# A hybrid convolution and S5 layer on one core: gelu in halves behind the sigmoids, one more buffer for each part of the gate, layer norms three to four steps earlier

## Chip, core and metric

The kernel runs on one core of a Trainium2 chip. The metric is the device time of one execution in microseconds (us). The kernel before has a median of 1850.74 us over three runs (1848.5 to 1852.46). TensorE (PE) does the matmuls, VectorE (DVE), ScalarE (ACT) and GpSimd (POOL) the elementwise work; SyncE (SP) issues every transfer (DMA) named here, one after the other. Each engine takes its instructions strictly in the order in which the program has them.

## What is computed

2048 positions of width 1024. The reference, cut to what matters here (the projections in front and the S5 scan itself are left out):

```python
p = split(h @ w_in)                       # val, glu gate, silu gate, u, silu gate: 5 x 1024 columns
# convolution branch
v = p0 * sigmoid(p1)
v = dwconv_latent(v, w, bias)             # 31 taps on a grid
v = silu(layernorm(v, ln_g, ln_b))
conv_out = v * silu(p2)
# S5 branch
y = gelu(y_f + y_b + d * u)               # y_f, y_b: the two scans, forwards and backwards
y = y * sigmoid(y @ glu_w + glu_b)
ssm_out = y * silu(p4)
mix = concat(conv_out, ssm_out) @ w_out
x = x + gate * mix
return rmsnorm(x, final_g)
```

## The kernel before

Activations lie with channels on the 128 partitions: 1024 channels are 8 channel tiles (`ct` or `k`, 0 to 7), and the positions are 4 blocks of 512 (`nb`). Each fp32 product is made of three passes: both operands are split in a high and a low part, and `mm3` (L133, L138, L139) adds high by high, high by low and low by high. A **product** below is 8 such triples, 24 matmuls of 512 columns, into one PSUM bank. All matmuls stand in one hand-made chain, each product's first one tied behind the last of the product before (`last`, `chain`), so that PE's order is the order of the code.

The stages follow each other: input projection with the convolution beside it (0 to about 700 us), S5 scan (to about 1243 us) with the last silu gates' columns projected between its parts, Glu stage (to 1436.6 us) and output stage (to the end).

- **End of the S5 stage.** For each group of channels ACT copies the transposed input operand `E` out of PSUM (L859), PE multiplies `S` from it (L892), DVE makes the state `H` (L904 to L927), PE reads it out as `Y` (L934, L943), and `ys` is written to DRAM as `y_d` (L947, L951). `activated(nb, ks)` loads channel tiles `ks` of `y_d` for one block (L1014), two to a buffer, applies gelu (L1021), rounds the high part `yh` (L1022) on ACT and makes the low part `yl` (L1023) on DVE. For block 0 that load has one buffer, for the others two. The silu gates leave PSUM as `gs` (L445).
- **Glu stage.** `project` makes one product `yh, yl` by `gwh, gwl` into `ps`, `gated(ct, nb, ps)` finishes it: loads the silu gate `gg` (L1112), adds `yf` = `yh` + `yl` (L1115), multiplies by `gg` (L1116), takes the sigmoid of `ps` into `gsg` on ACT (L1118), multiplies (L1119) and stores to `mix_d` (L1120). `ps` has few PSUM banks, so a product waits until an earlier `gsg` has read its bank. In block 0 the first five tiles (`EARLY`) project all but the last `k`, then the last one. The eight gelus of block 1 stand ahead of ct 5 of block 0, those of blocks 2 and 3 behind ct 1 of the block before.
- **Layer norms.** `layer_norm(nb)` is a generator of four steps: load `lx` and sum it on POOL (L1031 to L1036, `lsum`); the mean `mu` by a matmul (L1039), subtraction (L1042), squares (L1044, L1047) that POOL adds up (L1048, `lsq`); the variance `va` (L1052) and its inverse root `dg` on DVE; the root spread over the partitions `rb` (L1063), normalisation (L1068), silu (L1070), times the gate `lg` loaded pair by pair into one buffer (L1076, L1077), store to `mix_d` (L1078). The steps of block 0 run in the Glu stage behind the steps 8 * nb + ct named in `LN_STEPS`; those of blocks 1 to 3 in the output stage, four position tiles `t_` each, behind the half tiles of `LN_HALF`.
- **Output stage.** `w_out(i)` loads a row tile `wor` (L1000), rounds `woh` on ACT (L1001), and makes `wol` on POOL or DVE (L1002). Each position tile `t_` (16 of them) has four products `pso`: its S5 half (k8 = 1) times two column halves, then its convolution half. `mix_in` loads `mr` (L1097), `split_mix` makes `mh` on ACT (L1103) and `ml` on DVE (L1104). `evacuate` multiplies by the gate `gbc` and adds the input (L1177, L1178), `finish` applies the final norm with `fg` (L1189) and stores.

Order: the code runs under `tile.TileContext(schedule_with_timeline_sim=True)`, so a scheduler decides how ACT, DVE, POOL and SP interleave, within data dependencies and the hand-made ties.

Of the kernel before, what the change touches and what calls it, by code (L numbers as in the profile page):

```python
# [7 lines left out]
F32 = mybir.dt.float32  # L8
F32R = mybir.dt.float32r
I32 = mybir.dt.int32  # L10
AF = mybir.ActivationFunctionType
ALU = mybir.AluOpType
MUL, ADD, SUB = ALU.mult, ALU.add, ALU.subtract

P = 128
# [7 lines left out]
KT = D // P  # L23
NB = SEQ // 512
# [5 lines left out]
ROWS = SEQ // GRIDW  # L30
EPS = 1e-6

LN_STEPS = (6, 12, 16, 19)

LN_HALF = (0, 2, 4, 5)

H_LAST = (0, 2, 1, 3)

EARLY = 5
# [14 lines left out]
S_C, S_NG, S_BA, S_DW, S_DB, S_LG, S_LB, S_GB, S_D = 0, 16, 24, 48, 296, 304, 312, 320, 328  # L54
# [25 lines left out]
def build(ctx: ExitStack, tc: tile.TileContext, ins: dict, out: bass.AP):  # L80
# [705 lines left out]
    with tc.tile_pool(name="ss", bufs=2, reuse_waits="tile") as s2p, tc.tile_pool(name="ss1", bufs=1, reuse_waits="tile") as s1p, \  # L786
# [35 lines left out]
        def inputs(b):  # L822

            g0 = G * b
            gs_ = slice(g0, g0 + G)
            h2 = slice((b % 2) * G, (b % 2) * G + G)
            if b % 2 == 0:
                B_ = KBs[b // 2]
                KB = KBs[b // 2] = [s2p.tile([P, 4, GH], F32, tag=f"KB{i}", name=f"KB{i}") for i in range(2)]
                kt = s1p.tile([P, 4, GH], F32, tag="kt", name="kt")  # L830
                a = kbr[:, g0:g0 + 4].unsqueeze(2).to_broadcast([P, 4, GH])
                c = kbi[:, g0:g0 + 4].unsqueeze(2).to_broadcast([P, 4, GH])
                pt(KB[0], B_[0], a, op=MUL)
                pt(kt, B_[1], c, op=MUL)
                pt(KB[0], KB[0], kt, op=SUB)
                pt(KB[1], B_[0], c, op=MUL)
                pt(kt, B_[1], a, op=MUL)
                pt(KB[1], KB[1], kt, op=ADD)
            KB = KBs[b // 2]
            l = [t_[:, gs_].unsqueeze(3).to_broadcast(shp) for t_ in (lre, lim)]  # L840
            a = [t_[:, h2].unsqueeze(2).to_broadcast(shp) for t_ in KB]
            X = [s1p.tile(shp, F32, tag=f"X{i}", name=f"X{i}") for i in range(2)]
            xp = s1p.tile(shp, F32, tag="xp", name="xp")
            pt(X[0], a[0], l[0], op=MUL)
            pt(xp, a[1], l[1], op=MUL)
            pt(X[0], X[0], xp, op=SUB)
            pt(X[1], a[0], l[1], op=MUL)
            pt(xp, a[1], l[0], op=MUL)
            pt(X[1], X[1], xp, op=ADD)
            et = mm.tile([P, G, 2, P], F32, tag="mm", name="et")  # L850
            for g in range(G):
                for i in range(2):
                    m = nc.tensor.transpose(et[:, g, i], X[i][:, g].rearrange("p j h -> p (j h)"), ident)
                    if g == 0 and i == 0:
                        chain(m)
            last[0] = m
            k = blk[b]
            k.E = s1p.tile([P, G, 2, P], F32, tag="E", name="E")
            act(k.E, et, AF.Copy)  # L859

        def frame(b):

# [141 lines left out]
    def activated(nb, ks=range(KT)):  # L1004

        for k in ks:
# [11 lines left out]
                y_, (hi, lo) = y2[:, k % 2], yy[k, nb]  # L1018
            else:
                continue  # L1020
            act(y_, y_, AF.Gelu_apprx_tanh)  # L1021
            act(hi, y_, AF.Copy)  # L1022
            vt(lo, y_, hi.bitcast(F32), op=SUB)  # L1023

# [83 lines left out]

    def gated(ct, nb, ps):

        gt = gp.tile([P, 512], F32, tag="gg", name="gg")
        nc.sync.dma_start(gt, sg_d[ct][:, nb * 512:(nb + 1) * 512])  # L1112
        yf = gp.tile([P, 512], F32, tag="yf", name="yf")
        hi, lo = yy[ct, nb]
        vt(yf, hi.bitcast(F32), lo.bitcast(F32), op=ADD)  # L1115
        vt(yf, yf, gt, op=MUL)  # L1116
        sg = gp.tile([P, 512], F32, tag="gsg", bufs=1, name="gsg")
        act(sg, ps, AF.Sigmoid, bias=sml[:, S_GB + ct:S_GB + ct + 1])  # L1118
        vt(yf, yf, sg, op=MUL)  # L1119
        nc.sync.dma_start(mixed(nb, KT + ct), yf.rearrange("p (t q) -> p t q", q=P))  # L1120
        if 8 * nb + ct in LN_STEPS:
            next(lns[0])
# [12 lines left out]
    activated(0, [KT - 1])  # L1135
    for ct in range(EARLY):
        gated(ct, 0, project(gw[ct], yy, 0, [KT - 1], pss[ct]))
    activated(1)
    for ct in range(EARLY, KT):
        gated(ct, 0, project(gw[ct], yy, 0))  # L1140
    for nb in range(1, NB):
        for ct in range(KT):
            gated(ct, nb, project(gw[ct], yy, nb))
            if ct == 1 and nb + 1 < NB:
                activated(nb + 1)
            if nb == 2 and ct == 0:
                gbc = lp.tile([P, 1024], F32, name="gbc")
                fg = lp.tile([P, 1024], F32, name="fg")
                nc.sync.dma_start(gbc, gate_d[0:1].broadcast_to([P, 1024]))
                for row in (gate_d[1:2], ins["b_gate"]):  # L1150
                    nc.sync.dma_start(fg, row.broadcast_to([P, 1024]))
                    vt(gbc, gbc, fg, op=ADD)
                nc.sync.dma_start(fg, ins["final_g"].broadcast_to([P, 1024]))
            if nb == NB - 1:
                if ct == 0:
                    first = {hf: split_mix(mix_in(0, hf), hf) for hf in (1, 0)}
# [9 lines left out]
    with tc.tile_pool(name="op", bufs=2, reuse_waits="tile") as op:  # L1166
# [14 lines left out]
        def finish(t_, cols, xt, sq):  # L1181
# [6 lines left out]
            for cs_ in [slice(0, 1024)] if t_ < 15 else [slice(0, 512), slice(512, 1024)]:  # L1188
                st(xt[:, cs_], xt[:, cs_], rs, fg[:, cs_], op0=MUL, op1=MUL)  # L1189
                nc.sync.dma_start(ov[row(t_)[0], row(t_)[1], cs_], xt[:, cs_])  # L1190

        mrs = [None, None]
        for t_ in range(16):
            pool = mm if t_ % 2 == 0 else ops
# [15 lines left out]
            for k8 in (1, 0):  # L1210
# [6 lines left out]
                if t_ < 15:  # L1217
                    for i in range(2):
                        product(k8, i)
                        if k8 == 0:  # L1220
                            evacuate(i, cols[i], pss[i], xt, sq)
                if t_ < 12 and 2 * (t_ % 4) + 1 - k8 in LN_HALF:
                    next(lns[t_ // 4 + 1])
            if t_ == 15:
                for i in range(3):
                    product(1, i)
# [78 lines left out]
```

## Time and profile before

| | |
|---|---|
| median of three runs (lowest, highest) | 1850.74 us (1848.5, 1852.46) |
| the profiled execution | 1840.61 us, span 1838.8 us |
| PE busy | 1729.1 us, 94% of the span |
| DVE, ACT, POOL busy | 1422.2, 588.9, 602.9 us |
| granted TensorE clock, mean | 0.973 |
| Glu stage in the span | 1243 to 1436.6 us |
| output stage in the span | 1436.6 to 1838.8 us |

The span runs from the first to the last instruction; the execution's own time has about 2 us more. PE is close to always busy, so the first thing to look at is what stands between its matmuls: the waits listed for PE, each with the instruction that released it, and the stretches in which the clock column (PEclk, share of full speed) is below 1.00, because a matmul takes longer there.

### The profile page before, as it was taken

Reading aid. Unit: us, or ns where it says so; the run is one execution under the profiler, and the core shown is the slowest. Engines: PE = TensorE matmul, PEld = TensorE weight load, DVE = VectorE, ACT = ScalarE, POOL = GpSimd, SP = SyncE. Lnnn points to the kernel's source line nnn. Section 1 sums busy time; section 2 is a strip of 40 time slices with the busy share of each in tenths; the row PEclk is TensorE's granted clock in tenths of the full one; section 3 lists DMA queues with packets and bytes.
Section 4 is the critical chain, followed back from the end, with each engine's and each line's share of the span. In section 5 each row is a group of like instructions: output and inputs, shape, how many; then the busy total and the mean of one; then the engine's idle time right before and its main releaser. Section 6 shows DMA issues by size and latency. Waiting matters only on the chain.

```text
span 1838.8 us, 23677 instructions
## 1 busy us (share of the span) xinstructions
PE 1729.1 (94%) x8712; PEld 1363.7 (74%) x8712; DVE 1422.2 (77%) x2055; ACT 588.9 (32%) x905; POOL 602.9 (33%) x565
## 2 busy tenths in 40 slices
PE   7799799999999998999999999988999898989998
PEld 2675577787778886777777777777877686877877
DVE  6772799999998897999999999976575565555633
ACT  4442221221122123333443443454444322222211
POOL 1642244343342116556456464302022332213000
PEclk9899899999999998999999999999999999999999
DMA  9604121222222113333333333367549627363431
GB/s 351 211 18 125 33 104 53 94 78 80 69 99 86 57 63 108 116 109 104 111 108 118 114 95 117 101 214 222 148 122 284 225 92 215 106 177 120 130 123 46
DMA packets 175724, 227.45 MB, mean 124 GB/s; under 512 B 38516, under 2 KB 117492, under 8 KB 174584
## 3 DMA queue, kind: packets, MB, share of 16 engines
q1 hardware_dynamic: 175608, 225.94, 38.4%
q8 instruction: 69, 1.13, 0.3%
q14 instruction: 47, 0.39, 0.1%
HBM read 147.36 MB, written 78.52 MB: 123 GB/s over the span
## 4 chain that ended last, share of the span: by engine, by line
PE 53%; DVE 27%; DMA 10%; issue 4%; ACT 3%; SPq 2%; POOL 1%; DVEq 0%; ACTq 0%; POOLq 0%
PE ps L133 9%; PE ps L138 9%; PE ps L139 9%; DVE fQ L336 5%; PE pso L139 4%; PE pso L133 4%; PE pso L138 4%; DVE fR L336 4%; DVE fP L336 4%; PE S L892 3%; DMA mix_d<-yf 3%; DMA lg<-cg_d 3%; PE Y L943 3%; DMA y<-y_d 2%; PE Y L934 1%
## 5 line engine op out<-in xcount | busy, mean ns | idle before, releaser
L133 PE MATMUL ps<-hi,whi 128*128 128x512 f32 x1248 | 499.5, 400 | 1.2 <-ACT v L296 1.2
L138 PE MATMUL ps<-lo,whi 128*128 128x512 f32 x1248 | 492.0, 394 | 0.1
L139 PE MATMUL ps<-hi,wlo 128*128 128x512 f32 x1248 | 489.5, 392 | 0.0
L133 PEld LDWEIGHTS ps<-hi,whi 128*128 128x128 f32 x1248 | 235.6, 189 | 62.9 <-issue 10.2
L139 PEld LDWEIGHTS ps<-hi,wlo 128*128 128x128 f32 x1248 | 235.3, 189 | 53.8 <-issue 1.7
L138 PEld LDWEIGHTS ps<-lo,whi 128*128 128x128 f32 x1248 | 235.9, 189 | 52.7 <-issue 4.3
L133 PE MATMUL pso<-woh,mh 128*128 128x512 f32 (+1 forms) x528 | 209.2, 396 | 19.9 <-ACT mh L1103 13.8
L138 PE MATMUL pso<-wol,mh 128*128 128x512 f32 (+1 forms) x528 | 205.6, 389 | 2.3 <-DVE wol L1002 1.4
L139 PE MATMUL pso<-woh,ml 128*128 128x512 f32 (+1 forms) x528 | 206.3, 391 | 0.6 <-DVE ml L1104 0.5
L244 POOL TENSOR_TENSOR wlo<-wraw,whi 128x1024 fp32r<-128x1024 f32 x37 | 97.8, 2642 | 169.1 <-ACT whi L243 169.0
L336 DVE SCALAR_TENSOR_TENSOR fQ<-v,sml,fQ 128x960 f32<-128x960 f32 (+11 forms) x120 | 149.5, 1246 | 0.0
L336 DVE SCALAR_TENSOR_TENSOR fP<-v,sml,fP 128x960 f32<-128x960 f32 (+10 forms) x112 | 121.1, 1082 | 26.0 <-ACT fP L319 25.9
L133 PEld LDWEIGHTS pso<-woh,mh 128*128 128x128 f32 x528 | 101.1, 192 | 42.7 <-ACT mh L1103 15.1
L336 DVE SCALAR_TENSOR_TENSOR fR<-fS,comb,fR 128x960 f32<-128x960 f32 (+11 forms) x120 | 128.1, 1068 | 0.0
L916 DVE TENSOR_TENSOR_SCAN t<-mag,t 128x287 f32<-128x287 f32 x128 | 120.5, 1000 | 0.0
L138 PEld LDWEIGHTS pso<-wol,mh 128*128 128x128 f32 x528 | 101.1, 192 | 25.0 <-DVE wol L1002 2.2
L139 PEld LDWEIGHTS pso<-woh,ml 128*128 128x128 f32 x528 | 100.9, 191 | 23.7 <-DVE ml L1104 2.5
L133 PE MATMUL ps<-yh,gwh 128*128 128x512 f32 x256 | 102.6, 401 | 11.5 <-ACT gsg L1118 11.5
L243 ACT ACTIVATE whi<-wraw 128x1024 fp32r<-128x1024 f32 x37 | 39.0, 1055 | 211.6 <-PE ps L138 157.4
L138 PE MATMUL ps<-yl,gwh 128*128 128x512 f32 x256 | 101.1, 395 | 0.0
L139 PE MATMUL ps<-yh,gwl 128*128 128x512 f32 x256 | 100.9, 394 | 0.0
L1177 DVE TENSOR_TENSOR tm<-pso,gbc 128x512 f32<-128x512 f32 (+1 forms) x33 | 22.2, 674 | 91.5 <-PE pso L139 79.6
(298 smaller groups left out, 2845.1 us busy)
## 6 DMA issues: line engine op xcount, KB each, us to landing
wraw<-in_w_in SPq DMA_DIRECT2D x37, 512.0 KB
mr<-mix_d SPq DMA_DIRECT2D x32, 512.0 KB
wa<-in_w_ada SPq DMA_DIRECT2D x32, 256.0 KB
xt<-in_x_t SPq DMA_DIRECT2D x32, 256.0 KB
u_d<-us SPq DMA_DIRECT2D x32, 256.0 KB
f_d<-ff SPq DMA_DIRECT2D x32, 256.0 KB
cv_d<-v SPq DMA_DIRECT2D x8, 1024.0 KB
cg_d<-gs SPq DMA_DIRECT2D x32, 256.0 KB
```

What stands on the lines that cost most here:

```text
L133: i = nc.tensor.matmul(ps, wh, rh, start=first, stop=False)
L138: nc.tensor.matmul(ps, wh, rl, start=False, stop=False)
L139: last[0] = nc.tensor.matmul(ps, wl, rh, start=False, stop=end)
L243: act(hi, raw, AF.Copy)
L244: pt(lo, raw, hi.bitcast(F32), op=SUB)
L336: yield st(at(acc, lo_ + o, hi_ + o), at(src, lo_ + j, hi_ + j), tap[n](j), at(acc, lo_ + o, hi_ + o), op0=MUL, op1=ADD)
L892: m = nc.tensor.matmul(Sf[h_, o + c0:o + c1], k.E[:, d, i, h_], seq[g][d][:, c0:c1], start=True, stop=True, skip_group_check=True)
L916: nc.vector.tensor_tensor_scan(dst[:, d, 0:L], mag8[:, g0 + d:g0 + d + 1].to_broadcast([P, L]), src[:, d, 0:L], 0.0, op0=MUL, op1=ADD)
L934: m = nc.tensor.matmul(Y[:, g], k.M[:, g], k.U[:, g, NX:NCOL], start=True, stop=False, skip_group_check=True)
L943: m = nc.tensor.matmul(Y[:, g], k.F[h_, i, d], hs, start=False, stop=(i == 1 and d == 1), skip_group_check=True)
L1177: vt(tm, ps, gbc[:, cs_], op=MUL)
```

## The change

The gelus are tied behind an earlier ACT instruction, `late.g`: the last copy of `E`, and later the last sigmoid. The gelus of one block come in two halves of four channel tiles: block 1's behind the sigmoids of ct 4 and ct 5 of block 0, those of blocks 2 and 3 behind ct 1 and ct 3 of the block before. `gg` and `yf` get a third buffer, `gsg` a second. `gbc` and `fg`, loaded and added in the Glu stage before, are loaded at the head of the output stage. `LN_STEPS` and the output stage's table, which now counts products instead of pairs of products (`LN_QUARTER`; the old half steps 0, 2, 4, 5 are quarters 1, 5, 9, 11), name earlier places. No arithmetic changes.

```diff
-LN_STEPS = (6, 12, 16, 19)
-
-LN_HALF = (0, 2, 4, 5)
+LN_STEPS = (3, 8, 12, 15)
+
+LN_QUARTER = (0, 4, 7, 9)
...
-            act(k.E, et, AF.Copy)
+            late.g = act(k.E, et, AF.Copy)
...
-            act(y_, y_, AF.Gelu_apprx_tanh)
+            g_ = act(y_, y_, AF.Gelu_apprx_tanh)
+            tc.add_manual_dep(g_.ins, late.g.ins.name, mybir.DependencyInfo(
+                mybir.DependencyClass.NoSync, mybir.DependencyReason.DATA), reason="order")
...
-        gt = gp.tile([P, 512], F32, tag="gg", name="gg")
+        gt = gp.tile([P, 512], F32, tag="gg", bufs=3, name="gg")
...
-        yf = gp.tile([P, 512], F32, tag="yf", name="yf")
+        yf = gp.tile([P, 512], F32, tag="yf", bufs=3, name="yf")
...
-        sg = gp.tile([P, 512], F32, tag="gsg", bufs=1, name="gsg")
-        act(sg, ps, AF.Sigmoid, bias=sml[:, S_GB + ct:S_GB + ct + 1])
+        sg = gp.tile([P, 512], F32, tag="gsg", name="gsg")
+        late.g = act(sg, ps, AF.Sigmoid, bias=sml[:, S_GB + ct:S_GB + ct + 1])
...
-    activated(1)
     for ct in range(EARLY, KT):
+        if ct < KT - 1:
+            activated(1, range(4 * (ct - EARLY), 4 * (ct - EARLY) + 4))
         gated(ct, 0, project(gw[ct], yy, 0))
     for nb in range(1, NB):
         for ct in range(KT):
             gated(ct, nb, project(gw[ct], yy, nb))
-            if ct == 1 and nb + 1 < NB:
-                activated(nb + 1)
-            if nb == 2 and ct == 0:
-                gbc = lp.tile([P, 1024], F32, name="gbc")
-                fg = lp.tile([P, 1024], F32, name="fg")
-                nc.sync.dma_start(gbc, gate_d[0:1].broadcast_to([P, 1024]))
-                for row in (gate_d[1:2], ins["b_gate"]):
-                    nc.sync.dma_start(fg, row.broadcast_to([P, 1024]))
-                    vt(gbc, gbc, fg, op=ADD)
-                nc.sync.dma_start(fg, ins["final_g"].broadcast_to([P, 1024]))
+            if ct in (1, 3) and nb + 1 < NB:
+                activated(nb + 1, range(2 * ct - 2, 2 * ct + 2))
...
+        gbc = op.tile([P, 1024], F32, bufs=1, name="gbc")
+        fg = op.tile([P, 1024], F32, bufs=1, name="fg")
+        nc.sync.dma_start(gbc, gate_d[0:1].broadcast_to([P, 1024]))
+        for g1 in (gate_d[1:2], ins["b_gate"]):
+            nc.sync.dma_start(fg, g1.broadcast_to([P, 1024]))
+            vt(gbc, gbc, fg, op=ADD)
+        nc.sync.dma_start(fg, ins["final_g"].broadcast_to([P, 1024]))
...
-                if t_ < 12 and 2 * (t_ % 4) + 1 - k8 in LN_HALF:
-                    next(lns[t_ // 4 + 1])
+                        if t_ < 12 and 4 * (t_ % 4) + 2 * (1 - k8) + i in LN_QUARTER:
+                            next(lns[t_ // 4 + 1])
```

How the instructions moved, at three places. `y_10380`, `y_10388` and `y_10396` are the three pairs of channel tiles of block 0, in this order. ACT at the end of the S5 stage, up to the last copy of `E`, before:

```order
L445 ACTIVATE gs<-ps 128x512
L1021 ACT_TABLE_LOAD
L1021 ACTIVATE y_10388<-y_10388 128x1024
L1022 ACTIVATE yh<-y_10388 128x1024
L947 ACTIVATE ys<-Y 128x512
L868 ACTIVATE cs<-cst,frq 128x288 x2
L869 ACTIVATE cs<-cs,cst 128x288 x2
L1021 ACTIVATE y_10396<-y_10396 128x1024
L1022 ACTIVATE yh<-y_10396 128x1024
L445 ACT_TABLE_LOAD
L445 ACTIVATE gs<-ps 128x512
L859 ACTIVATE E<-et 128x512
```

and of the change, from the last copy of `E`:

```order
L859 ACTIVATE E<-et 128x512
L874 ACTIVATE sn<-sn 128x576
L1021 ACT_TABLE_LOAD
L1021 ACTIVATE y_10380<-y_10380 128x1024
L1024 ACTIVATE yh<-y_10380 128x1024
L445 ACT_TABLE_LOAD
L445 ACTIVATE gs<-ps 128x512
L947 ACTIVATE ys<-Y 128x512
L1021 ACT_TABLE_LOAD
L1021 ACTIVATE y_10388<-y_10388 128x1024
L1024 ACTIVATE yh<-y_10388 128x1024
L445 ACT_TABLE_LOAD
```

The last copy of `E` stood behind the gelus of all three pairs; now it stands ahead of the first of them, and the three pairs follow later than before.

ACT where the Glu stage's first sigmoids stand. `y_10650`, `y_10658` are the second half of block 1, `y_10856`, `y_10864` the first half of block 2. Before:

```order
L1021 ACTIVATE y_10650<-y_10650 128x1024
L1022 ACTIVATE yh<-y_10650 128x1024
L1021 ACTIVATE y_10658<-y_10658 128x1024
L1022 ACTIVATE yh<-y_10658 128x1024
L1021 ACTIVATE y_10856<-y_10856 128x1024
L1021 ACTIVATE y_10864<-y_10864 128x1024
L1118 ACT_TABLE_LOAD
L1118 ACTIVATE gsg<-ps,sml 128x512 x7
```

Of the change, where `y_10654`, `y_10662` are block 1's first half and `y_10704`, `y_10712` its second:

```order
L1120 ACT_TABLE_LOAD
L1120 ACTIVATE gsg<-ps,sml 128x512 x5
L1021 ACT_TABLE_LOAD
L1021 ACTIVATE y_10654<-y_10654 128x1024
L1021 ACTIVATE y_10662<-y_10662 128x1024
L1024 ACTIVATE yh<-y_10654 128x1024
L1024 ACTIVATE yh<-y_10662 128x1024
L1120 ACT_TABLE_LOAD
L1120 ACTIVATE gsg<-ps,sml 128x512
L1021 ACT_TABLE_LOAD
L1021 ACTIVATE y_10704<-y_10704 128x1024
L1024 ACTIVATE yh<-y_10704 128x1024
```

Six pairs of gelus stood ahead of the first sigmoid there; now five sigmoids come first, and a sigmoid stands between the halves.

DVE in the output stage, a layer norm's last step (`dg` to the gate's products), before:

```order
L176 SCALAR_TENSOR_TENSOR dg<-cst,nrxy 128x512
L1177 TENSOR_TENSOR tm<-pso,gbc 128x512
L1178 TENSOR_TENSOR ox<-tm,ox 128x512
L1177 TENSOR_TENSOR tm<-pso,gbc 128x512
L1178 TENSOR_TENSOR ox<-tm,ox 128x512
L1068 TENSOR_TENSOR lx<-lx,rb 128x512 x8
L1104 TENSOR_TENSOR ml<-mr,mh 128x1024
```

and of the change:

```order
L176 SCALAR_TENSOR_TENSOR dg<-cst,nrxy 128x512
L71 TENSOR_TENSOR orsp<-orsp,osq 128x1
L72 SCALAR_TENSOR_TENSOR orsy<-orsp,orsy 128x1
L1184 SCALAR_TENSOR_TENSOR ox<-ox,orsy,fg 128x1024
L1070 TENSOR_TENSOR lx<-lx,rb 128x512 x8
L1106 TENSOR_TENSOR ml<-mr,mh 128x1024
L1079 TENSOR_TENSOR lx<-lx,lg 128x512 x2
```

The normalisation (now L1070) stood behind the two evacuations of the third position tile; now it stands ahead of them, behind the finish of the second.

## Rows read from the trace of the kernel before

**Rows 1.** The page: span, then busy time, share and instructions of each engine.
```profile
span 1838.8 us, 23677 instructions
PE 1729.1 (94%) x8712; PEld 1363.7 (74%) x8712; DVE 1422.2 (77%) x2055; ACT 588.9 (32%) x905; POOL 602.9 (33%) x565
```
**Rows 2.** Windows by stage: stretch, length, busy us of each engine, PEclk, DMA share, GB/s.
```profile
1174.00:1243.00 69.00, 62.50 (x351) 49.05 (x350) 53.71 (x74) 37.82 (x52) 9.18 (x9) 0.98 0.57 182
1243.00:1436.60 193.60, 182.06 (x786) 148.45 (x786) 118.50 (x148) 87.85 (x100) 35.41 (x19) 0.97 0.64 199
1436.60:1839.00 402.40, 370.74 (x1639) 301.61 (x1638) 210.41 (x446) 96.92 (x154) 71.84 (x46) 0.96 0.43 133
```
**Rows 3.** Waits of PE, 1174 to 1839: us in total, times, longest.
```profile
PE pso L133 <- ACT mh L1103: 13.8, 3, 5.7
PE ps L133 <- ACT gsg L1118: 11.5, 4, 6.2
PE S L892 <- ACT E L859: 6.5, 2, 5.1
PE pso L133 <- ACT woh L1001: 6.1, 2, 3.8
PE pso L138 <- DVE wol L1002: 1.4, 2, 0.9
PE pso L138 <- POOL wol L1002: 0.9, 1, 0.9
PE pso L139 <- DVE ml L1104: 0.5, 1, 0.5
```
**Rows 4.** Windows of stretches behind such waits, and of an undisturbed product (PEclk 1.00).
```profile
1216.86:1220.37 3.51, 3.51 (x25) 2.55 (x25) 3.27 (x6) 2.84 (x5) 0.00 (x0) 0.60 0.95 275
1276.59:1284.29 7.70, 7.70 (x25) 6.19 (x25) 5.34 (x8) 2.35 (x4) 0.00 (x0) 0.71 0.44 135
1284.29:1289.73 5.44, 5.44 (x26) 4.51 (x24) 3.28 (x5) 1.10 (x2) 0.00 (x0) 1.00 0.54 146
1359.50:1366.67 7.17, 7.17 (x24) 5.76 (x25) 5.81 (x17) 2.26 (x3) 0.00 (x0) 0.76 0.36 116
1447.73:1463.72 15.99, 7.60 (x26) 4.72 (x24) 6.74 (x8) 5.64 (x6) 3.51 (x2) 0.84 0.85 282
1463.72:1470.02 6.30, 6.30 (x25) 5.09 (x24) 1.47 (x3) 0.75 (x3) 3.79 (x3) 0.86 0.59 200
1555.51:1563.88 8.37, 8.33 (x25) 6.20 (x25) 3.10 (x2) 1.06 (x1) 3.41 (x2) 0.67 0.75 253
1750.71:1758.71 8.00, 7.47 (x25) 5.70 (x25) 2.43 (x2) 1.06 (x1) 0.00 (x0) 0.79 0.67 229
```
**Rows 5.** Timeline of ACT: start, us, line, operation; in brackets the idle time before it.
```profile
1212.27 1.06 ACT L1021 ACTIVATE y<-y 128x1024 f32<-128x1024 f32 x1 [4.86 <-DMA y<-y_d]
1216.22 0.59 ACT L859 ACTIVATE E<-et 128x512 f32<-128x512 f32 x1
...
1273.48 1.06 ACT L1021 ACTIVATE y<-y 128x1024 f32<-128x1024 f32 x1 [2.25 <-DMA y<-y_d]
1274.55 1.28 ACT L1118 ACT_TABLE_LOAD   x1
1275.85 0.69 ACT L1118 ACTIVATE gsg<-ps,sml 128x512 f32<-128x512 f32 x1
```
**Rows 6.** The critical chain in the output stage, block 1's layer norm: start, us, what.
```profile
1517.30 4.87 DVE lx L1068 x8
...
1545.94 3.06 DMA mix_d<-lx
1549.02 5.28 DMA mr<-mix_d
```
**Rows 7.** Timeline of PE and of POOL around the same layer norm's earlier steps.
```profile
1481.01 0.59 PE L1039 MATMUL mu<-lsum,cst 128*128 128x512 f32 x1
1484.10 10.96 POOL L1048 TENSOR_TENSOR lsq<-lsq,ls 128x512 f32<-128x512 f32 x7 [7.43 <-ACT ls L1047]
```

## Prediction

> **What bounds the kernel.** Page first: PE is busy for 1729.1 of 1838.8 us [rows 1], so only what stands between its matmuls, or stretches them, can be gained; the other engines count where PE waits for them. The windows by stage then say where the change can act at all: in the end of the S5 stage 6.5 of 69.0 us are without PE, in the Glu stage 11.5 of 193.6, in the output stage 31.7 of 402.4 [rows 2] (length less PE busy); of the last, some 9 us are the final evacuation and store, which the change leaves alone. Ahead of 1174 us the change moves nothing that PE waits for.
>
> The list of PE's waits names the releasers of the rest: 13.8 + 11.5 + 6.5 + 6.1 + 1.4 + 0.9 + 0.5 = 40.7 us [rows 3]. A second cost hides in the busy time. After some of these waits the granted clock is between the two levels of 1.2 and 2.4 GHz: a product that takes 5.44 us at 1.00 keeps PE busy for 7.70 us at 0.71 behind the Glu stage's first wait, and 8.33 at 0.67 behind a layer norm's [rows 4]. Summed over the windows, less 5.44 each: first sigmoid 2.26, a later one 1.73; start of the output stage 2.16 + 0.86; layer norms 2.89, about 2.8 for the second (no row here; taken near the first's), 2.03 for the third. The `S` behind the longest `E` wait costs 3.51 * (1 - 0.60) = 1.4. Together 16.1 us, so 56.8 us in waits and clock can be gained at most.
>
> **The change, part by part.** The sums start from the profiled execution (1840.61 us, 10.1 below the median); I take the gain off the median 1850.74.
>
> *E ahead of the gelus (S5 end).* PE waits 6.5 us twice for the copy of `E`, which stands behind gelus on ACT that wait for `y` loads: a gelu waited 4.86 us for its load, started at 1212.27, and the copy of `E` came at 1216.22 [rows 5]. With E ahead of all three pairs 6.5 + 1.4 = 7.9 us go. What is late next: block 0's pairs share one load buffer, so three chains of load, gelu (1.06 us [rows 5]), rounding and `yl` now run one behind the other, later, and SP issues the second and third load behind the eight `glu_w` tiles. DVE takes the third `yl` ahead of the steps that make the last `H`, so PE can wait for that at the last `Y`. No row shows this wait. Lower bound 0 (the chain fits), upper 6.3 (a load's wait of 4.86 with 1.4 of clock again). I take 3: walking the chain with a load every five microseconds leaves `H` about 2 us behind PE, and one such wait may lower the clock. Gain 5.
>
> *Sigmoids ahead of block 1's gelus (Glu).* The first sigmoid came at 1275.85, right behind gelus that waited for loads, the last by 2.25 us [rows 5]; PE waited up to 6.2 us there and 11.5 in all [rows 3]. Now five sigmoids come straight behind block 0 and no block needs its gelus less than two products after they are issued, block 1 excepted. The third `yf` and second `gsg` let ACT go on without waiting for DVE's product and the store. So 11.5 + 2.26 + 1.73 = 15.5 us go. New: block 1's second half needs two gelus, each behind a table load and a sigmoid of block 0. By the rows each costs 1.28 + 1.06 and a rounding taken as long as the gelu, 1.06, and a sigmoid with its load 1.28 + 0.69 [rows 5]: twice 5.4 us, about two products' 10.9. It just fits, and I take 1 (0, or 4 where one more load wait comes in). Gain 14.5.
>
> *Output stage's start.* Waits for `woh` and `wol` are 6.1 + 0.9 + 0.9 (one of the two DVE waits; the second, about 0.5, lies behind the next) + 0.5 = 8.4, with 3.0 of clock [rows 3, 4]. The last `wor` loads stand on SP behind block 0's layer norm. That layer norm ends some 4 steps of 5.44 us earlier, so the loads come about 20 us earlier against a stage that starts 20 us earlier, but are no longer queued behind the norm's gate loads; the last wait was 3.81 at its longest of two, so most goes. In exchange three transfers of `gbc` and `fg` and two additions now stand here: the first `evacuate` needs them. PE waits for an evacuation only two tiles later, when a PSUM bank is wanted again, so 20 us cover them. But DVE takes block 1's mean subtraction behind the first finish, which needs `fg`: cover a few us. I take 2 left over (0 to 6). Gain 9.4.
>
> *Layer norms in the output stage.* Each block ends in a chain: normalisation from 1517.30, gate loads, last store 1545.94 (3.06), load `mr` 1549.02 (5.28) [rows 6]; the matmul comes at 1555.5, 38.2 us behind the normalisation's start, and waited up to 5.7 us (13.8 for three blocks [rows 3]). `rb` moves two products up, 2 * 5.44 = 10.9 us, against a wait of 5.7. That leaves some 5 us of slack, so 13.8 + 0.5 + 2.89 + 2.8 + 2.03 = 22.0 go. Price: between mean and variance there are now three products (16.3 us) in place of four. That path took from 1481.01 to 1484.10 + 10.96 = 1495.06, 14.05 us [rows 7]: 2.3 us of slack. The sum `lsum` has four products ahead of `mu`, as before. I take 2 for a late `mu` or `va` (0 to 8). Gain 20.
>
> *Costed at nothing:* ACT's six additional table loads outside the chains above, at 1.28 us each beside an engine that is busy for 32% [rows 1, 5]; further buffers; the same loads and stores on SP, in another order.
>
> Against the change speaks a rule of the Trainium skill (ScalarE: Activation LUTs, "What ACT_TABLE_LOAD costs" and its advice to do all of one table set before switching): a switch is 1283 ns and about 1380 ns of drain, 2.66 us. The first figure agrees with the row's 1.28; the drain does not show, as the load started 0.01 us after the gelu's end and the sigmoid 0.02 after the load. By the page the three switches at the S5 end and the four in block 1's half would add 7 * 1.38 = 9.7 us, and the gain would be 39.
>
> Sum: 5 + 14.5 + 9.4 + 20 = 48.9 of 56.8. **Forecast: 1850.74 - 48.9 = 1801.8, say 1802 us** (a profiled execution of about 1792).
>
> **Rivals.**
> *A: ACT's chains stay in the way (S5 and Glu).* For: the y chain has one buffer, the sum of block 1's half is within half a us of its cover, and a gelu has waited up to 4.86 us. If each of the two regions gives back most of its gain by waits as long as today's, 17 of 19.5 us are lost: 1819. Against: the E copies and the first five sigmoids depend on no load.
> *B: the norm's wait only moves.* `mu` or `va` late by a few us in each block, or gate loads stretched since they now compete with other loads. Most of its gain lost, 20: 1822. Against: the bounds above, with positive slack everywhere.
> *C: table loads on the path.* Six more loads at 1.28 us, all on the path and none hidden: 7.7 us, 1810; with a clock loss behind three of them, 1815. Against: ACT's share of 32%. The page's rule, above, would make it 1812.
> *D: slower.* In PE's fixed order a matmul that is late holds everything behind it, and nine of them moved (`mu`, `va`, `rb` of three blocks). Each late as `mh` is today costs 5.7 + 2.9 = 8.6, nine 77: 1879. It decides from an average of 48.9 / 9 = 5.4 us, clock included. For: 14.05 us are to fit in 16.3 and POOL's part of it is 10.96. Against: it needs all nine, and `rb` follows `va` by two products as before.
> That the change does not do what it says is excluded for the order, which the rows of instructions show.
>
> **Chances.** Forecast (three or four regions gain as summed, 1793 to 1812) 0.62; A 0.20; B 0.10; C 0.03; D 0.04; no measurable change 0.01. Its lower end is the whole 56.8 (1794) with 2 us for the runs' own spread; the upper takes the upper bounds of two regions. To leave out no more than 2 in 10 the range reaches over A and B with a few us beyond: **1792 to 1826**. What can be told from no change is about 0.2%, 3.7 us. Faster 0.94 (forecast, A, B, C are 0.95, less 0.01 for a B and an A together), same 0.02, slower 0.04.
>
> **What would show it.** Right: no PE wait for `E`; the wait for `gsg` under 2 us; PE at clock 1.00 where the Glu stage starts; Glu stage shorter by about 15 us, its end near 1416; no wait for `mh` at three places in the output stage and under 4 us for `woh`, `wol`. Forecast wrong by A: waits for `H` or `yl` around the last `Y`, or for `yh` and `yl` at block 1's first products. By B: waits of `mu` for `lsum`, `va` for `lsq`, or `mh` again. By C: idle ACT time behind each table load. By D: nine waits of over 5 us on L1041, L1054 and L1065 of the changed kernel.

## The result, and the profile after

| | before | after |
|---|---|---|
| median of runs on the same chips (lowest, highest) | 1851.6 us (1848.5, 1853.68) | 1822.97 us (1818.01, 1826.13) |
| ratio, 95% interval | | 0.986, 0.9839 to 0.9881 |
| profiled execution, span | 1840.61, 1838.8 us | 1824.31, 1822.5 us |

The change makes the kernel about 26 us faster (22 to 30 by the interval); 48.9 were forecast, to 1802. The two traces differ by only 16.3 us: the profiled execution of before was at the low end of its kind, and the part ahead of the change varies from run to run (the fourth S from the last starts at 1160.48 before, at 1165.96 after, and between 1160 and 1167 in all fourteen traces of this study). So below each stage is measured from landmark to landmark.

The page of after, span and engines:

```profile
span 1822.5 us, 23694 instructions
PE 1727.3 (95%) x8712; PEld 1363.4 (75%) x8712; DVE 1422.7 (78%) x2055; ACT 594.4 (33%) x911; POOL 598.6 (33%) x565
```

The four stretches, as windows (length, busy time of each engine, PEclk, DMA share, GB/s): from the fourth `S` from the last to the first Glu product, the Glu stage, the first four products of the output stage, and its rest. Before, cut at the same landmarks:

```profile
1160.48:1242.85 82.37, 75.87 (x426) 59.75 (x424) 66.11 (x92) 42.56 (x61) 12.28 (x12) 0.98 0.53 167
1242.85:1436.62 193.77, 182.23 (x789) 148.60 (x787) 118.64 (x149) 88.00 (x100) 35.42 (x19) 0.97 0.64 199
1436.62:1470.02 33.40, 25.01 (x97) 18.93 (x97) 18.88 (x16) 10.15 (x13) 14.19 (x7) 0.90 0.66 214
1470.02:1838.84 368.82, 345.71 (x1543) 282.68 (x1541) 191.53 (x430) 86.77 (x142) 57.63 (x39) 0.97 0.41 126
```

After:

```profile
1165.96:1247.05 81.09, 77.27 (x427) 59.74 (x425) 65.35 (x91) 38.85 (x57) 11.98 (x12) 0.96 0.53 170
1247.05:1440.36 193.31, 181.93 (x789) 148.63 (x787) 121.42 (x152) 99.92 (x112) 38.89 (x20) 0.98 0.62 190
1440.36:1470.36 30.00, 24.72 (x98) 19.17 (x97) 12.65 (x12) 7.41 (x8) 7.61 (x5) 0.89 0.79 265
1470.36:1822.53 352.17, 340.01 (x1543) 279.95 (x1541) 191.88 (x433) 86.75 (x144) 57.92 (x40) 0.99 0.43 135
```

The gains are 1.3, 0.5, 3.4 and 16.6 us, together 21.8, where the prediction had 5, 14.5, 9.4 and 20. The output stage's layer norms gave nearly what was summed; the Glu stage gave almost nothing. The waits of PE after (they answer to [rows 3]):

```profile
PE ps L133 <- ACT gsg L1120: 10.0, 3, 5.1
PE pso L133 <- ACT woh L1001: 4.1, 1, 4.1
PE Y L934 <- ACT ys L947: 3.8, 1, 3.8
PE mu L1041 <- POOL lsum L1038: 3.5, 1, 3.5
PE ps L138 <- DVE yl L1025: 0.8, 1, 0.8
PE pso L138 <- POOL wol L1002: 0.7, 1, 0.7
PE ps L133 <- ACT yh L1024: 0.7, 1, 0.7
PE pso L138 <- DVE wol L1002: 0.5, 1, 0.5
```

The waits for `mh` and `E` are gone. The wait for `gsg` is nearly as large as before, 10.0 for 11.5: the first one (6.2 us) went, but two that stood before the change as well, at the 20th and the 28th product of the stage, are twice as long. Before, then after:

```profile
1359.50 0.70 PE L133 MATMUL ps<-yh,gwh 128*128 128x512 f32 x1 [2.23 <-ACT gsg L1118]
1408.41 0.50 PE L133 MATMUL ps<-yh,gwh 128*128 128x512 f32 x1 [2.59 <-ACT gsg L1118]
...
1360.05 0.56 PE L133 MATMUL ps<-yh,gwh 128*128 128x512 f32 x1 [4.34 <-ACT gsg L1120]
1411.43 0.70 PE L133 MATMUL ps<-yh,gwh 128*128 128x512 f32 x1 [5.14 <-ACT gsg L1120]
```

Before, the sigmoid of the first stood behind gelus that waited 4.55 and 0.83 us for `y`, that of the second behind a `woh` that waited 6.80 us for `wor`. New are `ys` and `lsum`. Windows behind four of these waits (`ys`, two of `gsg`, `lsum`) show the clock's part again:

```profile
1241.32:1247.05 5.73, 5.73 (x21) 3.74 (x21) 2.87 (x5) 1.52 (x3) 0.00 (x0) 0.50 0.56 166
1360.05:1367.22 7.17, 7.17 (x24) 5.76 (x25) 2.82 (x5) 7.10 (x7) 0.00 (x0) 0.76 1.00 295
1411.43:1418.60 7.17, 7.17 (x24) 5.75 (x25) 6.85 (x5) 3.24 (x5) 4.34 (x2) 0.76 0.49 183
1479.51:1487.60 8.09, 8.09 (x26) 5.85 (x27) 7.67 (x21) 3.12 (x6) 2.48 (x2) 0.79 0.42 137
```

A wait of 3.8 us is followed by a whole `Y` at 0.50, the level of 1.2 GHz, so it takes twice its time: 2.9 us on top. Behind `gsg` it is 7.17 - 5.44 = 1.7 each.

The wait for `ys`, on ACT: the third pair's load lands at 1237.35, and a table load (1.28 us), the gelu and the rounding stand between it and `ys`.

```profile
1237.35 1.28 ACT L1021 ACT_TABLE_LOAD   x1 [2.53 <-DMA y<-y_d]
1238.64 1.06 ACT L1021 ACTIVATE y<-y 128x1024 f32<-128x1024 f32 x1
1239.73 1.06 ACT L1024 ACTIVATE yh<-y 128x1024 fp32r<-128x1024 f32 x1
1240.69 0.58 ACT L947 ACTIVATE ys<-Y 128x512 f32<-128x512 f32 x1
```

**What holds the sigmoids now.** ACT's timeline at the first of the two places:

```profile
1341.03 0.69 ACT L1120 ACTIVATE gsg<-ps,sml 128x512 f32<-128x512 f32 x1 [6.37 <-DVE yf L1121]
1341.74 1.28 ACT L1072 ACT_TABLE_LOAD   x1
1352.95 5.05 ACT L1072 ACTIVATE lx<-lx,sml 128x512 f32<-128x512 f32 x7 [9.93 <-DVE lx L1070]
1358.02 1.28 ACT L1120 ACT_TABLE_LOAD   x1
1359.31 0.69 ACT L1120 ACTIVATE gsg<-ps,sml 128x512 f32<-128x512 f32 x1
```

Seven silus of block 0's layer norm stand ahead of a sigmoid and wait 9.93 us for the normalisation; PE goes on at 1360.05, when that sigmoid has read its bank. DVE's timeline says why the normalisation is late, though the matmuls of its `rb` started at 1338.3:

```profile
1340.25 0.68 DVE L1121 TENSOR_TENSOR yf<-yf,gsg 128x512 f32<-128x512 f32 x1
1344.54 0.69 DVE L1117 TENSOR_TENSOR yf<-yh,yl 128x512 f32<-128x512 f32 x1 [3.60 <-DMA mix_d<-yf]
...
1350.30 0.69 DVE L1117 TENSOR_TENSOR yf<-yh,yl 128x512 f32<-128x512 f32 x1 [3.74 <-DMA mix_d<-yf]
...
1352.24 4.86 DVE L1070 TENSOR_TENSOR lx<-lx,rb 128x512 f32<-128x512 f32 x8
```

Additions of `yf` for later steps stand ahead of it, and each waits for the store of `yf` that was just issued. At the second place a `woh` (L1001) that waits 8.47 us for `wor` stands ahead of the sigmoid:

```profile
1409.74 1.06 ACT L1001 ACTIVATE woh<-wor 128x1024 fp32r<-128x1024 f32 x1 [8.47 <-DMA wor<-in_w_out]
1410.70 0.67 ACT L1120 ACTIVATE gsg<-ps,sml 128x512 f32<-128x512 f32 x1
```

### The profile page after: what moved, and what is told of

It reads as the page before. It is cut to its first block, busy times and chain, and to the rows that moved or that the text cites. A ratio compares the mean times of both kernels' runs of the same rounds, so it can differ in the third digit from the quotient of the medians.

```text
span 1822.5 us, 23694 instructions
## 1 busy us (share of the span) xinstructions
PE 1727.3 (95%) x8712; PEld 1363.4 (75%) x8712; DVE 1422.7 (78%) x2055; ACT 594.4 (33%) x911; POOL 598.6 (33%) x565
## 4 chain that ended last, share of the span: by engine, by line
PE 57%; DVE 24%; DMA 8%; issue 4%; ACT 3%; POOL 2%; SPq 2%; DVEq 0%; ACTq 0%; POOLq 0%
PE ps L133 10%; PE ps L138 9%; PE ps L139 9%; PE pso L133 6%; PE pso L139 6%; PE pso L138 6%; DVE fQ L336 5%; DVE fR L336 4%; DVE fP L336 4%; DMA mix_d<-yf 3%; PE S L892 3%; PE Y L943 3%; PE Y L934 1%; DMA y<-y_d 1%; DMA wa<-in_w_ada 1%
## 5 line engine op out<-in xcount | busy, mean ns | idle before, releaser
L336 DVE SCALAR_TENSOR_TENSOR fQ<-v,sml,fQ 128x960 f32<-128x960 f32 (+11 forms) x120 | 153.3, 1277 | 0.0
L139 PEld LDWEIGHTS pso<-woh,ml 128*128 128x128 f32 x528 | 99.8, 189 | 21.8
L388 POOL TENSOR_TENSOR pp<-cc,lim 128x256 f32<-128x256 f32 x32 | 34.2, 1069 | 170.8 <-DVE ff L396 136.0
```

What stands on the lines that cost most here:

```text
L139: last[0] = nc.tensor.matmul(ps, wl, rh, start=False, stop=end)
L336: yield st(at(acc, lo_ + o, hi_ + o), at(src, lo_ + j, hi_ + j), tap[n](j), at(acc, lo_ + o, hi_ + o), op0=MUL, op1=ADD)
L388: pt(pp, ci, q, op=MUL)
```

## Experiments

The theory: the output stage's gain comes from its table alone, and the Glu stage's was lost because a sigmoid in ACT's fixed order stands behind work that waits for something else. The rival: the Glu stage is bound otherwise (its transfers, or the layer norm moved up into it), and each wait that goes comes back elsewhere. Ratios are to the kernel before on the same chip, with 95% intervals.

### The output stage's table alone

```diff
 # the kernel before
-LN_HALF = (0, 2, 4, 5)
+LN_QUARTER = (0, 4, 7, 9)
...
+                        if t_ < 12 and 4 * (t_ % 4) + 2 * (1 - k8) + i in LN_QUARTER:
+                            next(lns[t_ // 4 + 1])
```

> The kernel before with the output stage's earlier layer-norm steps alone (quarters 0, 4, 7, 9), nothing of the Glu stage. Theory (the gain that was measured is the output stage's, from these steps): no wait of PE for mh, output stage shorter by 14 to 22 us, time 1829 to 1838; gbc and fg being loaded in the Glu stage here, block 1's mean should not wait for its sum (0 to 1 us, 3.5 in the changed kernel). Rival (the steps pay only because the Glu stage's rearrangement makes the loads behind them earlier): mh still waits, or mu, va or rb waits in its place, time above 1843.

Measured: 0.9895 (0.9867 to 0.9923), 1826.33 us. Output stage behind its first four products:

```profile
1474.03:1822.27 348.24, 338.41 (x1543) 279.10 (x1541) 191.15 (x430) 86.02 (x142) 56.62 (x40) 0.99 0.42 133
```

348.24 for 368.82: 20.6 us, with no wait for `mh`; the time is a little below the theory's 1829 to 1838. This table alone carries most of what the whole change gained; block 1's mean waits 1.2 us here, a little over the theory's 0 to 1.

### The Glu stage's part alone

```diff
 # the changed kernel
-LN_STEPS = (3, 8, 12, 15)
+LN_STEPS = (6, 12, 16, 19)
-LN_QUARTER = (0, 4, 7, 9)
+LN_QUARTER = (1, 5, 9, 11)
```

> The changed kernel with both layer-norm tables as before (steps 6, 12, 16, 19; quarters 1, 5, 9, 11). Theory (in the Glu stage the first sigmoid's wait went, but ACT's order holds later sigmoids, behind the silus of block 0's layer norm and behind w_out roundings that wait for their loads): Glu stage 188 to 194 us as in both kernels, two waits for gsg of 2 to 6 us behind silus and behind woh, and the three waits for mh back; time 1838 to 1850. Rival (the Glu stage gives nothing since the layer norm was moved up into it): with the old steps the Glu stage falls by 10 us or more, to under 184 us.

Measured: 0.9935 (0.9916 to 0.9954), 1835.26 us, below the theory's interval. The Glu stage and the output stage's rest:

```profile
1246.71:1438.26 191.55, 181.67 (x789) 148.50 (x788) 119.61 (x155) 96.66 (x109) 34.34 (x19) 0.98 0.61 193
...
1463.64:1837.93 374.29, 346.93 (x1543) 282.84 (x1541) 193.85 (x433) 87.26 (x144) 60.34 (x41) 0.97 0.41 128
```

The Glu stage stays at 191.6, so the earlier steps of block 0's layer norm are not what cost it; one wait for `gsg` of 5.8 us (its sigmoid stands behind gelus that waited 7.8 us for `y`, and behind silus) and one of `rb` of 1.9 are there, not two for `gsg`. The gain is in the output stage's first products, 25.4 us for 33.4. The waits for `mh` are back (16.8 us for 13.8), and the rest of the output stage takes 5.5 us more than before the change.

### A fourth buffer for yf

```diff
-        yf = gp.tile([P, 512], F32, tag="yf", bufs=3, name="yf")
+        yf = gp.tile([P, 512], F32, tag="yf", bufs=4, name="yf")
```

> The changed kernel with a fourth buffer for yf. Theory (the normalisation of block 0 stands on DVE behind three additions that each wait for the store of the step before, since three yf buffers leave no slack; the silus behind it hold the sigmoid): the additions behind the variance no longer wait for stores, the normalisation starts within 3 us of rb instead of 13, the wait for gsg of 4.3 us behind the silus goes with its 1.7 us of clock, Glu stage 5 to 7 us shorter, time 1815 to 1819. Rival (the stage is bound by its transfers, at 0.64 of the DMA engines' time): the waits move elsewhere and the Glu stage stays at 192 to 195 us, time 1820 to 1826.

Measured: 0.9854 (0.9829 to 0.9879), 1819.04 us; Glu stage 193.5 us. DVE's timeline at the same place:

```profile
1343.04 0.69 DVE L1117 TENSOR_TENSOR yf<-yh,yl 128x512 f32<-128x512 f32 x1 [3.65 <-DMA mix_d<-yf]
...
1348.69 0.69 DVE L1117 TENSOR_TENSOR yf<-yh,yl 128x512 f32<-128x512 f32 x1 [3.63 <-DMA mix_d<-yf]
```

That step of the theory falls: with four buffers the scheduler only places the additions one step further ahead, and each still waits for the newest store. Counted in DVE's timelines, 14 steps had their last product when the 17th addition waited (1344.54 above); with four buffers it is the 18th (1343.04). The number of buffers isn't what makes the normalisation late; the order is.

### The additions behind the normalisation

```diff
         for ct in range(KT):
-            vt(xs[ct], xs[ct], rb, op=MUL)
+            late.n = vt(xs[ct], xs[ct], rb, op=MUL)
...
-        vt(yf, hi.bitcast(F32), lo.bitcast(F32), op=ADD)
+        y_ = vt(yf, hi.bitcast(F32), lo.bitcast(F32), op=ADD)
+        if late.n is not None:
+            tc.add_manual_dep(y_.ins, late.n.ins.name, mybir.DependencyInfo(
+                mybir.DependencyClass.NoSync, mybir.DependencyReason.DATA), reason="order")
```

> The changed kernel with the yf additions of later steps tied behind block 0's normalisation on DVE. Theory (those additions wait for a store each and stand ahead of the normalisation however many buffers yf has, as four of them showed; the silus and, behind them, a sigmoid are late by that): the normalisation starts within 3 us of rb instead of 13, the wait for gsg of 4.3 us behind the silus goes, or falls under 1.5 us, Glu stage 186 to 189 us, time 1815 to 1819. Rival (the silus hold the sigmoid by their own 7 us with the table loads, whenever they come): a wait of 3 us or more remains behind them and the Glu stage stays at 191 to 195 us.

Measured: 0.9772 (0.9737 to 0.9807), 1806.44 us. The Glu stage's window, and the normalisation and silus in the timelines:

```profile
1245.87:1425.50 179.63, 177.54 (x789) 146.34 (x787) 121.92 (x152) 101.03 (x113) 39.82 (x20) 1.00 0.66 206
```

```profile
1342.45 4.87 DVE L1070 TENSOR_TENSOR lx<-lx,rb 128x512 f32<-128x512 f32 x8
...
1343.16 5.06 ACT L1072 ACTIVATE lx<-lx,sml 128x512 f32<-128x512 f32 x7
```

The normalisation starts 4.9 us behind `rb` (1337.55) in place of 13.9, more than the theory's 3, and the stage is still shorter than its 186 to 189 us. No wait of PE for `gsg` is left in the Glu stage, not the one behind `woh` either: with block 0's layer norm done earlier the w_out loads come earlier too. The fifth `woh`, the one that held the sigmoid, starts 148.6 us into the stage (1394.48) in place of 162.7. 193.31 to 179.63 is 13.7 us from one tie, and the kernel with block 1's later mean, below, has 178.97 with it. With the same transfers at a higher rate (206 GB/s for 190), the rival is out: they don't bind the stage.

### That tie without the change's own tie

```diff
 # the kernel with the normalisation tie
             g_ = act(y_, y_, AF.Gelu_apprx_tanh)
-            tc.add_manual_dep(g_.ins, late.g.ins.name, mybir.DependencyInfo(
-                mybir.DependencyClass.NoSync, mybir.DependencyReason.DATA), reason="order")
```

> The version whose yf additions are tied behind the normalisation, without the change's tie of the gelus behind late.g (halves, buffers and tables stay). ACT's order is then as before the change: gelus of block 0 ahead of E, six pairs ahead of the first sigmoid. Theory (the tie is worth the first sigmoid's wait in the Glu stage and nothing at the S5 end, where it trades a wait for E for one for ys): the waits for E return and that for ys goes, S5 stretch 80 to 83 us; a wait for gsg of 5 to 7 us with 2 us of clock at the sixth product, Glu stage 185 to 189 us; time 1812 to 1818. Rival (the normalisation was all of the Glu stage's cost): Glu stage within 3 us of 179.6; time under 1810.

Measured: 0.9901 (0.9879 to 0.9923), 1827.49 us, worse than either expected.

```profile
1249.89:1446.58 196.69, 184.31 (x788) 151.08 (x787) 117.66 (x151) 87.91 (x101) 38.39 (x20) 0.96 0.63 187
```

The Glu stage is at 196.7: the first sigmoid's wait (6.3 us) is back, and one of 4.2 us behind it. So the change's tie was right and needed; it could not pay before the next thing in the queue had moved. Neither tie alone gives anything in this stage (193.3 and 196.7 for 193.8 before), both give 14 us. At the S5 end the waits for `E` are back (6.1 us) and that for `ys` is gone, in 83.2 us for 79.7 with the tie and 82.4 before the change: there it mostly trades one wait for another.

### The buffers and gbc, fg as before

```diff
 # the kernel with the normalisation tie
-        gt = gp.tile([P, 512], F32, tag="gg", bufs=3, name="gg")
+        gt = gp.tile([P, 512], F32, tag="gg", name="gg")
...
-        yf = gp.tile([P, 512], F32, tag="yf", bufs=3, name="yf")
+        yf = gp.tile([P, 512], F32, tag="yf", name="yf")
...
-        sg = gp.tile([P, 512], F32, tag="gsg", name="gsg")
+        sg = gp.tile([P, 512], F32, tag="gsg", bufs=1, name="gsg")
```

(and `gbc`, `fg` at nb 2, ct 0 of the Glu stage, as before the change).

> The version whose yf additions are tied behind the normalisation, with the buffers of gg, yf and gsg back to 2, 2 and 1, and gbc and fg loaded in the Glu stage again. Theory (the buffers are what lets ACT and DVE run ahead of the stores, as the prediction put it; the late sum in block 1 comes from the gbc and fg loads in the output stage): Glu stage 4 to 10 us longer than the 179.6 with waits for gsg back, block 1's wait for lsum under 1.5 us; time 1806 to 1814. Rival (the store round trip sets the pace whatever the buffers, as the fourth yf buffer showed, and the sum is late from the w_out loads): Glu stage within 3 us of 179.6 and the wait for lsum 2.5 us or more; time 1802 to 1810.

Measured: 0.9841 (0.9814 to 0.9868), 1815.44 us; Glu stage 188.4 us, wait for `lsum` 1.3 us.

```profile
1243.08:1431.49 188.41, 180.53 (x788) 146.78 (x786) 123.21 (x152) 96.52 (x110) 37.91 (x19) 0.98 0.68 205
```

With fewer buffers the Glu stage takes 8.8 us more, as the theory had it, though the longest wait shows at `yh` (4.9 us) rather than at `gsg` (1.5 at most). This run also has the loads of `gbc` and `fg` back in that stage, so the share of the buffers alone is not shown. And `lsum` is late by about 2.5 us more with `gbc` and `fg` in the output stage.

### The first mh later

```diff
-                if ct == 0:
-                    first = {hf: split_mix(mix_in(0, hf), hf) for hf in (1, 0)}
+                if ct == 5:
+                    first = {hf: split_mix(mix_in(0, hf), hf, late.g) for hf in (1, 0)}
```

(`split_mix` ties `mh` behind its third argument.)

> The changed kernel with the two mh roundings of the output stage's first tile tied behind the sigmoid of ct 5 of the last block. Theory (ACT waits 6 us for mr there with three woh roundings behind it; so the w_out buffers come free late, the next loads are late, and a woh that waits 8.5 us for one holds a sigmoid): the wait for gsg of 5.1 us behind woh goes with 1.7 us of clock, the waits for woh and wol at the output stage's start fall from 5.3 to under 2 us, time 1811 to 1816. Rival (the w_out loads are late because block 0's layer norm holds their buffers and SP's queue): woh still waits for its load ahead of a sigmoid, the wait of PE stays above 3 us, time 1820 to 1826.

Measured: 0.9878 (0.9847 to 0.991), 1823.62 us.

```profile
PE pso L139 <- DVE ml L1109: 12.1, 1, 12.1
```

Half of each: the wait for `gsg` behind `woh` went and the Glu stage fell to 186.5 us, but `ml` now stands on DVE behind `yf` additions that wait for stores, and PE waits 12.1 us for it. The gain went there whole: the output stage's first products take 36.6 us in place of 30.0.

### The three edits together

> The changed kernel with these three edits together. Theory: the three gains add up, 5 + 6 + 9 less a third, the Glu stage 180 to 183 us, time 1804 to 1812. Rival (each wait that goes uncovers the next one on the same queues): Glu stage above 188 us, time above 1815.

Measured: 0.9836 (0.9806 to 0.9866), 1817.28 us, worse than the normalisation tie alone (1806.44). PE waits 4.0 us for the late `ml` and 6.3 for `lsum`. The time is the rival's; the Glu stage, at 184.8, lies between the two, without a wait for `gsg`. Why it takes 5.1 us more than with the normalisation tie alone was not followed up.

### One pair of gelus free, then two

```diff
-            tc.add_manual_dep(g_.ins, late.g.ins.name, mybir.DependencyInfo(
...
+            if nb or k > 1:
+                tc.add_manual_dep(g_.ins, late.g.ins.name, mybir.DependencyInfo(
...
```

> The changed kernel with block 0's first pair of gelus not tied behind the last copy of E; the other pairs stay tied. Theory (one load buffer makes three loads and gelus follow one another only after the last E; the third one holds ys and H, and PE waits at the last Y): the second pair is loaded ahead of the glu_w tiles, the third pair's gelu comes by 1230 instead of 1238, PE's wait of 3.8 us for ys goes, with 2.8 us of clock in Y: 4 to 7 us less between the S5 stage's end and the Glu stage's start; time 1816 to 1820. E must not wait again (under 1 us). Rival (the y loads are late because of what shares the DMA engines, the glu_w tiles): the third pair still lands at 1235 or later and PE waits 2 us or more; time 1820 to 1826.

Measured: 0.986 (0.983 to 0.9891), 1821.04 us; stretch 82.6 us. The third pair's gelu comes at 1226.7, in time, but the wait for `ys` is 3.8 us again: now the fourth gelu stands ahead of `ys`. E waits 1.4 us again.

With `k > 3` in place of `k > 1`:

> The changed kernel with the first two pairs of block 0's gelus free of the tie and the third pair behind the last copy of E. Theory (PE waits at the S5 end because the pairs follow one another behind the last E, and the third load stands behind the 4 MB of glu_w; freeing one pair was not enough, since the fourth gelu then stood ahead of ys): the third pair is loaded ahead of glu_w, the last E is copied by 1207, neither E (under 1.5 us) nor ys holds PE, and the stretch from the last but three S to the first Glu product falls from 81.1 to 74 to 77 us; time about 1817. Rival (whichever order, one load buffer and ACT's order cost PE 6 to 8 us here): the stretch stays at 80 to 83 us.

Measured: 0.9856 (0.9826 to 0.9885), 1819.24 us; stretch 80.5 us, with waits for E (1.4) and for `H` (1.9 and 0.9). The rival: each order costs PE about the same here. (The Glu stage is at 189.9 us in this run, 3.4 less than with the change; no run says why.)

### Block 1's mean one product later

```diff
 # the kernel with the normalisation tie
-                        if t_ < 12 and 4 * (t_ % 4) + 2 * (1 - k8) + i in LN_QUARTER:
+                        if t_ < 12 and 4 * (t_ % 4) + 2 * (1 - k8) + i in (LN_QUARTER if t_ > 3 else (0, 5, 8, 10)):
```

> The version whose yf additions are tied behind the normalisation, and block 1's mean, variance and root one product later (quarters 0, 5, 8, 10); blocks 2 and 3 as in the change. Theory (the sum of block 1 is late since its lx loads stand behind the last w_out loads, and PE waits 3.9 us for it with some clock behind): one product later the wait for lsum goes or falls under 0.5 us, no wait for mh comes back (chain of 38 us against seven products of 5.5), output stage 3 to 6 us shorter, time 1800 to 1804. Rival (the late sum costs PE again at the variance, or mh is late): a wait of 2 us or more at va, rb or mh in block 1, no gain, 1804 to 1809.

Measured: 0.9763 (0.9735 to 0.9791), 1800.64 us; its output stage:

```profile
1449.83:1797.50 347.67, 338.47 (x1543) 279.02 (x1541) 193.02 (x433) 86.77 (x144) 57.98 (x41) 0.99 0.43 137
```

As the theory had it, the wait for `lsum` is gone, no other came (`ml` 0.5 us), and the stage is 5.1 us shorter in the trace. By the runs the intervals of this kernel, the one with the normalisation tie alone and the next one overlap; this one has the lowest median of the study.

### ys and H ahead of the third pair

```diff
 # the last kernel; late.y is the ys copy of the last Y but one, late.h the last H
+            if nb == 0 and k == 5:
+                tc.add_manual_dep(g_.ins, late.y.ins.name, mybir.DependencyInfo(
+                    mybir.DependencyClass.NoSync, mybir.DependencyReason.DATA), reason="order")
+                tc.add_manual_dep(l_.ins, late.h.ins.name, mybir.DependencyInfo(
+                    mybir.DependencyClass.NoSync, mybir.DependencyReason.DATA), reason="order")
```

> The version with the normalisation tie and block 1's later mean, and in it the third pair of block 0: its gelu tied behind the ys copy of the last Y but one, its yl on DVE behind the last H. Theory (at the S5 end PE waits since that gelu, waiting for its load, stands ahead of ys on ACT and its yl ahead of H on DVE): PE waits neither for ys nor for H (under 1 us at the last Y), the stretch from the last but three S to the first Glu product falls from 81.0 to 74 to 76 us; the Glu stage may give back 2 to 3 us where the first product now waits for the last pair's yl; time 1796 to 1799. Rival (the chain of loads through one buffer sets the end, whichever of the two engines shows it): the first Glu product waits for yl by as much as was saved, both stretches together stay within 1.5 us of 260.0, time 1799 to 1804.

Measured: 0.9773 (0.9753 to 0.9793), 1805.56 us. S5 end and Glu stage:

```profile
1163.05:1237.32 74.27, 74.27 (x427) 58.22 (x425) 63.97 (x89) 36.48 (x54) 11.98 (x12) 1.00 0.56 176
1237.32:1426.47 189.15, 181.06 (x789) 148.34 (x787) 122.65 (x155) 103.28 (x116) 37.18 (x20) 0.97 0.64 202
```

PE waits for nothing at the S5 end, 6.8 us less, and the Glu stage takes 10.2 us more: its first product runs through the three pairs and then waits 5.7 us for the `yh` of the seventh channel tile, whose load lands at 1244.4, with the clock behind. Both together are 263.4 us for 260.0. The rival was right, and short of the cost: PE meets what is late at one product or another. That the chain of loads through block 0's one buffer sets this end fits all four orders tried, but is not shown, as no run gave it a second buffer. The output stage's first four products took 23.87 us here for 29.74, so that the traced executions end up about alike (1799.4 and 1797.5 us); by the medians this kernel is no faster.

## Why the prediction came out as it did

It was right in its direction and its range, and wrong by 21 us in its value. By the traces 27.1 of the 48.9 us are missing; the medians show less, since the forecast took its gain off the median of before, and the traced execution lay 10.1 us below that. Step by step, by the traces:

- *What bounds the kernel* held: nearly all that was gained or lost is PE's waits and the clock behind them.
- *Layer norms in the output stage*, 20: 16.6 came, and 20.6 where this table was tried alone. The mechanism was right with its slack: no `mh` wait, no late `va` or `rb`. The price was mis-sized: `mu` of block 1 waited 3.5 us with 1.7 of clock, 5.2 where 2 were taken. The prediction compared the distance between sum and mean (four products, as before) but not that the `lx` loads stand behind the w_out and now the `gbc` and `fg` loads.
- *Sigmoids ahead of block 1's gelus*, 14.5: 0.5 came. **This is the step that failed.** Its first half held: the first sigmoid's 6.2 us went, and block 1's half costs 1.4 us, with the clock at 1.00, where 1 was taken. What failed is the sentence that all 11.5 us go since the buffers let ACT go on. It asked which gelus stand ahead of a sigmoid, and not what else does: the silus, which wait for DVE, and `woh`, which waits for a load. The second stood there before the change, as the list of ACT's waits then said (21.0 us for `wor`). So 8.5 us of wait and clock went at the first sigmoid, and 4.7 more of wait at the 20th and 28th products, 1.7 more of clock and 1.4 for block 1's half came. With the additions moved behind the normalisation the stage gave 13.7 us more: the predicted size was there, one more edit away.
- *E ahead of the gelus*, 5: 1.3 came. The waits for E went as said; the wait at the last `Y` came as said too, but 3.8 us with 2.9 of clock in place of 3 altogether. Its releaser is `ys` on ACT, which the prediction did not have in its chain; DVE's last `H` was late as well (1244.0), as it had it, though PE didn't get to wait for that.
- *Output stage's start*, 9.4: 3.4 came. The `wor` loads wait on SP for buffers that `wol` (8.8 us between 1370 and 1480) and block 0's layer norm (3.8) free late, so most of the wait for `woh` and `wol`, 5.3 of 8.4, stayed; 25.4 us for these products in place of 30.0, in the Glu part alone, show that it could be had.

By mechanism this is rival A, at 0.20: ACT's chains stay in the way, 17 us lost in these two regions to 1819 by its sum; 17.7 were lost. That the measured 1823 lies near 1819 is partly luck, as the other two regions lacked 9.4 more and the medians hide some of it. B was a part of it (`mu`). C did not come as the sum of six loads, but single loads do stand on the path: a table load of 1.28 us falls into the wait of 3.8 for `ys`, as the lines above show, and another stands between the silus and the sigmoid that PE waits for. On their cost by the Trainium skill (ScalarE: Activation LUTs, "What ACT_TABLE_LOAD costs", 1283 ns and a drain of about 1380): after the silus end at 1358.00 the load runs 1.28 us from 1358.02 and the sigmoid starts at 1359.31, so the drain doesn't show here either. D did not come: one of the nine moved matmul groups waited.

## What to carry to other kernels

A tie that takes one late instruction out of an in-order queue gives only as much as the next one in that queue allows: list everything ahead of the awaited instruction, on its engine and on the engine that feeds it, and what each of them waits for. An added buffer does not reorder a queue; a scheduler may use it to run one step further ahead and wait for the newest store as before. Where every order of the engines gives about the same time, as at the S5 end here, ordering only chooses where the wait shows; look then at what feeds them all (here perhaps the loads through one buffer, which no run changed).

## What was not expected of the hardware

While POOL makes two `wol` (1397.93 to 1403.24 in the trace of after), an addition and a product of DVE take about four times their usual 0.69 us:

```profile
1398.13 2.85 DVE L1117 TENSOR_TENSOR yf<-yh,yl 128x512 f32<-128x512 f32 x1
1401.02 2.77 DVE L1118 TENSOR_TENSOR yf<-yf,gg 128x512 f32<-128x512 f32 x1
...
1397.93 5.31 POOL L1002 TENSOR_TENSOR wol<-wor,woh 128x1024 fp32r<-128x1024 f32 x2 [78.77 <-ACT woh L1001]
```

That is about the length of one `wol` on POOL each, as if the two engines took turns. The Trainium skill says so (SBUF — State Buffer, "SBUF: two separate sides"): of an operation of DVE with two SBUF inputs and one of POOL that reads SBUF, the one that starts first holds a shared pair of ports for its whole instruction, and the other waits. The rows agree with it; no run here tried it by itself.
